# Weights of a two-layer mixer in half tiles: three half places for raw weights, five for low halves, and a low half made from the high half

## The chip, the cores and the metric

The kernel runs on one core of a Trainium2 chip. The metric is the device time of one execution in microseconds. Five engines work side by side and wait for each other by semaphores: TensorE (PE, with its weight loads as PEld), VectorE (DVE), ScalarE (ACT), GpSimd (POOL) and SyncE (SP). Besides them, DMA engines move data between memory and the core; the DMAs of this kernel are issued from the queues of SP and POOL.

## The reference, cut to what matters

Two layers, each of three sublayers with a residual: a gated feed-forward (FFN), a mixing sublayer (Mix), a second FFN. Sequence 512, width 1024, FFN width 2816, all in float32.

```python
for l in range(DEPTH):
    h = swiglu_ffn(rmsnorm(x, ffn1_pre_g[l]), ffn1_w_gu[l], ffn1_w_down[l])
    x = x + 0.5 * rmsnorm(h, ffn1_post_g[l])
    h = mixing_sublayer(rmsnorm(x, mix_pre_g[l]), w_in[l], ...)
    x = x + rmsnorm(h, mix_post_g[l])
    h = swiglu_ffn(rmsnorm(x, ffn2_pre_g[l]), ffn2_w_gu[l], ffn2_w_down[l])
    x = x + 0.5 * rmsnorm(h, ffn2_post_g[l])

def mixing_sublayer(h, ...):
    z = h @ w_in
    uv, pz, qz, kz, vz, qi, ki, wi, cz, gz = jnp.split(z, ...)
    branches = (gmlp_mixer(uv, ...), pool_mixer(pz, ...),
                sparse_attention(qz, kz, vz, qi, ki, wi, rel_bias), conv_mixer(cz, ...))
    gates = jax.nn.sigmoid(gz.reshape(B, S, N_BRANCH, D_MODEL))
    y = sum over n of gates[:, :, n] * (branches[n] @ w_branch[n])
    return y @ w_out

def conv_mixer(ab, dw, db, ln_g, ln_b):      # 31 taps, causal, one filter for each of 256 channels
    a, gt = jnp.split(ab, 2, axis=-1)
    h = a * jax.nn.sigmoid(gt)
    h = lax.conv_general_dilated(h, dw[:, None, :], padding=[(CONV_K - 1, 0)], ...) + db
    return jax.nn.silu(layernorm(h, ln_g, ln_b))
```

## The kernel before

**Products in three parts.** TensorE multiplies in a reduced float32 format. So each operand is split into a high half, the value rounded to that format, and a low half, what is left; a product is wH·xH + wL·xH + wH·xL. The activations lie with features on 128 partitions and the 512 positions along the free axis: eight tiles xH and eight xL. A weight is a tile of 128x1024, eight 128x128 blocks; with it goes one `gemm` (L263) of 24 matmuls of 512 columns, in the order of `mm3s` (L241): for the first seven blocks wH·xH and wL·xH by turns, then wH·xL, then the last block. Thus the first matmul with the low half is the second of the gemm. All of them are recorded with line L253, whatever the stage; the matmuls of the first four weights of a sublayer, its head, have L287.

**Weights.** Each of some 400 weights comes in through `weights()` (L180). SP issues the load of the raw tile (L184) into one of two places of the pool "raw", each 128x1024; ACT copies it to the high half wH (L197). For the low half wL there are three ways:

- in the FFNs, and for the first two gemms behind the head (`ahead_weight`) and the last four of Mix, VectorE subtracts: wL = raw − wH (L202);
- with `far=True`, ACT copies the raw tile with a scale of −1 into wL (L199), which rounds it to the negated high half, and a DMA from POOL's queue adds the weight from memory onto it (L200), which leaves the low half. The tile of the low half is complete when this adding DMA lands. So are made: the weights of Mix behind the head (`col`, L629: positions, gates), the branch weights `w_branch`, the first half of `w_out`, and weights 1 to 3 of a head that follows a sublayer boundary;
- with `ring=True`, the first weight of such a head: two tiles of 128x512 each for high and low half out of the pool "h"; POOL subtracts (L191).

wH has four places of 128x1024 and wL four. A place is free again when the last matmul that reads it has ended.

**Gates.** In `gates` (L749) the four branches follow each other in the order 1, 0, 3, 2. For each of eight output tiles one gate weight (24 matmuls) and two blocks of a branch weight (6 matmuls) go through TensorE; one branch weight serves four output tiles, and so holds its places for four rounds. VectorE normalises the gate's result (L756), ACT makes a tanh of it (L757), VectorE multiplies with the branch's result (L766) and POOL or VectorE adds (L768).

**Beside it.** The attention (scores, top-k on VectorE in L934 and L935, softmax on ACT in L953 to L959, L984), the convolution (31 operations a channel tile on VectorE, L865) and the other branches are generators; `pump` runs a piece of them at each gemm. `conv` works on the tile "cv" of 512 + 30 columns, whose first 30 POOL sets to zero (L699). At a sublayer boundary VectorE makes statistics (L300 to L322) for a matmul (L330) that all of the next scaling waits for.

**What sets the order.** The Python code records instructions in the order of a plan; a list scheduler then sets the order of each engine's queue by its own estimates, keeping data and buffer dependencies. In stretches marked `pinned` the weights keep program order (`pin`, L205). An engine works off its queue strictly in order.

Of the kernel before, what the change touches and what calls it, by code (L numbers as in the profile page):

```python
# [11 lines left out]
F32 = mybir.dt.float32  # L12
F32R = mybir.dt.float32r
I32 = mybir.dt.int32
AF = mybir.ActivationFunctionType
ALU = mybir.AluOpType
AX = mybir.AxisListType

P = 128
N = 512  # L20
# [29 lines left out]
class Builder:  # L50
# [65 lines left out]
    def late_consts(self):  # L116
# [13 lines left out]
        oh = self.t([P, 1024], F32, "raw", 2)  # L130
# [8 lines left out]
    def late_consts2(self):  # L139
        nc, sb, dr = self.nc, self.sb, self.a["rlin"]  # L140
        rev = self.t([P, 4, 256], F32, "raw", 2)
        nc.sync.dma_start(rev, bass.AP(tensor=dr.tensor, offset=dr.offset, ap=[[1, P], [384, 4], [1, 256]]))
        anti = self.tmp(w=P)
        nc.gpsimd.memset(anti, 0.0)
        nc.gpsimd.affine_select(out=anti, in_=anti, pattern=[[1, P]], compare_op=ALU.not_equal, fill=1.0,
                                base=-(P - 1), channel_multiplier=1)
        self.tb = sb.tile([P, 4, 256], F32, name="tb")
        for j in range(2):
            pj = self.pt("st")
            nc.tensor.matmul(pj, anti, rev[:, 2 * j:2 * j + 2, :], start=True, stop=True)  # L150
            nc.scalar.activation(self.tb[:, 2 * j:2 * j + 2, :], pj, AF.Copy)
# [27 lines left out]

    def weights(self, src, n, ring=False, raw=None, far=False):  # L180

        nc = self.nc
        raw = raw or self.t([P, 1024], F32, "raw", 2)
        nc.sync.dma_start(raw[:, :n], src)  # L184
        if ring:
            hs, ls = [], []
            for i in range(2):
                h, lo = self.ring(), self.ring()
                r = raw[:, i * N:(i + 1) * N]
                nc.scalar.activation(h, r, AF.Copy)  # L190
                nc.gpsimd.tensor_tensor(lo, r, h.bitcast(F32), op=ALU.subtract)  # L191
                hs.append(h)
                ls.append(lo)
            return hs, ls
        h = self.t([P, 1024], F32R, "wH", 4)
        lo = self.t([P, 1024], F32R, "wL", 4)
        self.pin(nc.scalar.activation(h[:, :n], raw[:, :n], AF.Copy))  # L197
        if far:
            self.pin(nc.scalar.activation(lo[:, :n], raw[:, :n], AF.Copy, scale=-1.0))  # L199
            nc.gpsimd.dma_start(lo[:, :n], src, accum_op=ALU.add)  # L200
            return h, lo
        self.pin(nc.vector.tensor_tensor(lo[:, :n], raw[:, :n], h.bitcast(F32)[:, :n], op=ALU.subtract))  # L202
        return h, lo
# [362 lines left out]
class Mix:  # L566
# [33 lines left out]
    def params(self):  # L600
        b, nc, l, a = self.b, self.b.nc, self.l, self.b.a

        raw = b.t([P, 1024], F32, "raw", 2)
# [16 lines left out]
        raw = b.t([P, 1024], F32, "raw", 2)  # L620
# [30 lines left out]
    def rest(self):  # L651
# [42 lines left out]
        for j in range(2):  # L694
            zg = self.norm(T_CZ + 2 + j)
            nc.scalar.activation(zg, zg, AF.Tanh, scale=0.5)
            za = self.norm(T_CZ + j, scale=0.5)
            hp = b.t([P, N + CONV_K - 1], F32, "cv", 2)
            nc.gpsimd.memset(hp[:, 0:CONV_K - 1], 0.0)  # L699
            nc.vector.scalar_tensor_tensor(hp[:, CONV_K - 1:], zg, 1.0, za, op0=ALU.add, op1=ALU.mult)  # L700
            self.hpad.append(hp)
# [152 lines left out]
    def conv(self):  # L854
# [3 lines left out]
        for j in range(2):  # L858
# [3 lines left out]
            nc.vector.tensor_scalar(a, hp[:, 0:N], dw(0), b.v(l, V_CB + j), op0=ALU.mult, op1=ALU.add)  # L862
            yield 450
            for t in range(1, CONV_K):
                nc.vector.scalar_tensor_tensor(a, hp[:, t:t + N], dw(t), a, op0=ALU.mult, op1=ALU.add)  # L865
                if t % 2 == 0:
                    yield 1360
# [200 lines left out]
```

## Time and profile before

| | us |
|---|---|
| median of 3 runs (2332.76 to 2336.97) | 2333.0 |
| the profiled execution, its own time | 2332.65 |
| its span, first to last instruction | 2330.9 |
| PE busy | 2283.6 |
| DVE busy | 1193.7 |
| ACT busy | 927.4 |
| POOL busy | 276.6 |

The first layer takes roughly 0 to 380 us (FFN1), 380 to 790 (Mix) and 790 to 1165 (FFN2), the second 1165 to 1545, 1545 to 1950 and 1950 to 2331. The busy time of an engine is a sum over its instructions; the queries by stage and by wait tell where TensorE stands still and for whom. "x <- y" in a wait means that x stood until y had ended. A DMA's row shows its issue; when it lands is given apart.

### The profile page before, as it was taken

Reading aid. Unit: us, or ns where it says so; the run is one execution under the profiler, and the core shown is the slowest. Engines: PE = TensorE matmul, PEld = TensorE weight load, DVE = VectorE, ACT = ScalarE, POOL = GpSimd, SP = SyncE. Lnnn points to the kernel's source line nnn. Section 1 sums busy time; section 2 is a strip of 40 time slices with the busy share of each in tenths; the row PEclk is TensorE's granted clock in tenths of the full one; section 3 lists DMA queues with packets and bytes.
Section 4 is the critical chain, followed back from the end, with each engine's and each line's share of the span. In section 5 each row is a group of like instructions: output and inputs, shape, how many; then the busy total and the mean of one; then the engine's idle time right before and its main releaser. Section 6 shows DMA issues by size and latency. Waiting matters only on the chain.

```text
span 2330.9 us, 28353 instructions
## 1 busy us (share of the span) xinstructions
PE 2283.6 (98%) x11158; PEld 1909.0 (82%) x11158; DVE 1193.7 (51%) x2144; ACT 927.4 (40%) x1390; POOL 276.6 (12%) x326
## 2 busy tenths in 40 slices
PE   8999999999999999999999999999999999999997
PEld 7888889777888988888888888887778889888886
DVE  5333346799433552433573334468984336423345
ACT  5232224564554532222343222355545545322221
POOL 0000003311331200000110000032123312000001
PEclk9999999999999999999999999999999999999999
DMA  5333333867778433233333323347687773323322
GB/s 170 100 99 92 108 92 90 188 145 168 178 166 182 115 100 98 92 99 97 99 105 93 111 91 100 91 114 167 145 181 174 173 169 100 104 95 95 99 91 68
DMA packets 82557, 282.27 MB, mean 121 GB/s; under 512 B 9428, under 2 KB 13176, under 8 KB 82424
## 3 DMA queue, kind: packets, MB, share of 16 engines
q1 hardware_dynamic: 64136, 213.87, 28.5%
q0 software_dynamic: 18288, 66.59, 16.7%
q8 instruction: 87, 1.43, 0.2%
q14 instruction: 46, 0.38, 0.1%
HBM read 278.32 MB, written 2.10 MB: 120 GB/s over the span
## 4 chain that ended last, share of the span: by engine, by line
PE 85%; DVE 9%; ACT 2%; issue 2%; DMA 1%; POOL 0%; SPq 0%; POOLq 0%; DVEq 0%; ACTq 0%
PE mm L253 49%; PE at L253 31%; DVE ca L865 3%; PE mm L287 2%; PE at L287 1%; DMA wL<-in_w_in_dram 1%; DVE sc L935 1%; DVE t L402 1%; DVE m L934 1%; PE st L330 1%; PE st L314 1%; DVE x L405 1%; DVE xL L416 1%; ACT wH L197 0%; DVE t L646 0%
## 5 line engine op out<-in xcount | busy, mean ns | idle before, releaser
L197 ACT ACTIVATE wH<-raw 128x1024 fp32r<-128x1024 f32 (+1 forms) x394 | 407.4, 1037 | 836.8 <-issue 581.7
L253 PE MATMUL mm<-xH,wL 128*128 128x512 f32 x1344 | 525.9, 392 | 6.5 <-DMA wL<-in_w_in_dram 6.5
L253 PE MATMUL mm<-xH,wH 128*128 128x512 f32 x1344 | 530.5, 396 | 1.6 <-DVE t L756 1.3
L202 DVE TENSOR_TENSOR wL<-raw,wH 128x1024 fp32r<-128x1024 f32 (+1 forms) x272 | 324.3, 1194 | 255.9 <-ACT wH L197 255.7
L253 PE MATMUL mm<-h,wH 128*128 128x512 f32 (+1 forms) x1496 | 409.2, 354 | 0.3 <-DVE t L756 0.3
L253 PE MATMUL mm<-xL,wH 128*128 128x512 f32 x1344 | 359.0, 389 | 0.0
L253 PEld LDWEIGHTS mm<-xH,wL 128*128 128x128 f32 x1344 | 253.4, 189 | 61.7 <-DMA wL<-in_w_in_dram 9.4
L253 PEld LDWEIGHTS mm<-xH,wH 128*128 128x128 f32 x1344 | 253.3, 188 | 58.5 <-issue 4.2
L253 PEld LDWEIGHTS mm<-h,wH 128*128 128x128 f32 x1496 | 263.8, 188 | 41.8 <-DVE t L756 0.5
L253 PEld LDWEIGHTS mm<-xL,wH 128*128 128x128 f32 x1344 | 252.5, 188 | 52.6
L253 PE MATMUL at<-xH,wH 128*128 128x512 f32 x704 | 277.1, 395 | 7.3 <-ACT xH L223 6.7
L253 PE MATMUL at<-xH,wL 128*128 128x512 f32 x704 | 274.0, 391 | 0.0
L253 PE MATMUL mm<-h,wL 128*128 128x512 f32 (+1 forms) x748 | 252.4, 352 | 0.0
L253 PE MATMUL at<-h,wH 128*128 128x512 f32 (+1 forms) x776 | 219.6, 366 | 0.0
L199 ACT ACTIVATE wL<-raw 128x1024 fp32r<-128x1024 f32 x122 | 128.6, 1054 | 176.9 <-PE mm L253 144.9
L253 PE MATMUL at<-xL,wH 128*128 128x512 f32 x704 | 187.8, 389 | 0.0
L253 PEld LDWEIGHTS at<-xH,wH 128*128 128x128 f32 x704 | 132.9, 189 | 37.6 <-ACT xH L223 7.0
L253 PEld LDWEIGHTS at<-h,wH 128*128 128x128 f32 x776 | 140.4, 188 | 24.6
L253 PEld LDWEIGHTS mm<-h,wL 128*128 128x128 f32 x748 | 140.4, 188 | 20.3
L253 PEld LDWEIGHTS at<-xH,wL 128*128 128x128 f32 x704 | 132.7, 188 | 29.3 <-issue 1.4
L253 PEld LDWEIGHTS at<-xL,wH 128*128 128x128 f32 x704 | 132.2, 188 | 27.5
L253 PE MATMUL at<-h,wL 128*128 128x512 f32 (+1 forms) x388 | 136.5, 366 | 0.0
(212 smaller groups left out, 2300.8 us busy)
## 6 DMA issues: line engine op xcount, KB each, us to landing
raw<-in_ffn_w_gu_dram SPq DMA_DIRECT2D x173, 512.0 KB, 3.5
raw<-in_w_in_dram SPq DMA_DIRECT2D x98, 512.0 KB, 6.4
wL<-in_w_in_dram POOLq DMA_DIRECT2D x94, 512.0 KB, 7.1
raw<-in_ffn_w_down_dram SPq DMA_DIRECT2D x64, 448.0 KB, 3.3
raw<-in_ffn_w_down_dram SPq DMA_DIRECT2D x32, 512.0 KB, 3.5
raw<-in_w_branch_dram SPq DMA_DIRECT2D x16, 512.0 KB, 5.1
wL<-in_w_branch_dram POOLq DMA_DIRECT2D x16, 512.0 KB, 7.0
raw<-in_w_out_dram SPq DMA_DIRECT2D x16, 512.0 KB, 6.5
```

Source lines behind the costliest of these rows:

```text
L197: self.pin(nc.scalar.activation(h[:, :n], raw[:, :n], AF.Copy))
L199: self.pin(nc.scalar.activation(lo[:, :n], raw[:, :n], AF.Copy, scale=-1.0))
L202: self.pin(nc.vector.tensor_tensor(lo[:, :n], raw[:, :n], h.bitcast(F32)[:, :n], op=ALU.subtract))
L253: self.nc.tensor.matmul(out, w[a], m[b], start=(first and i == 0), stop=(last and i == 3 * n - 1))
L287: self.nc.tensor.matmul(out, w[a], m[b], start=(count[j] == 1), stop=(count[j] == 3 * KD))
L314: self.nc.tensor.matmul(ps[:, c - c0:c - c0 + 1], s[:, c * P:(c + 1) * P], self.ones[:, 0:1], start=(i == 0), stop=(i == len(tiles) - 1))
L330: self.nc.tensor.matmul(ps[:, s], self.ones, dg[:, s], start=True, stop=True)
L402: nc.vector.scalar_tensor_tensor(u[:, c], s.o[k][:, c], self.v(s.post[0], s.post[1] + k), pb[:, c], op0=ALU.mult, op1=ALU.mult)
L405: e.tensor_tensor(self.xt[k][:, c], self.xt[k][:, c], u[:, c], op=ALU.add)
L416: nc.vector.scalar_tensor_tensor(self.xl[k][:, c], self.xt[k][:, c], g, self.xh[k].bitcast(F32)[:, c], op0=ALU.mult, op1=ALU.subtract)
L865: nc.vector.scalar_tensor_tensor(a, hp[:, t:t + N], dw(t), a, op0=ALU.mult, op1=ALU.add)
L934: nc.vector.max(m8, sc[:, :W])
```

## The change

Raw weights land in half tiles: the pool "raw" has three places of 128x512 in place of two of 128x1024. A weight is then two loads, two copies to wH and, where VectorE subtracts, two subtractions. With `far`, one negation of the whole tile reads wH, no longer the raw tile, so that it comes behind both copies; the adding DMA is unchanged. The ring's low halves are made likewise by ACT and adding DMAs. wL has five places, wH still four. The convolution's tile has no padding and no memset; a tap s works on 512 − s columns. The bias constants (`late_consts2`) land in two half tiles.

```diff
+    def raw(self):
+        return self.t([P, N], F32, "raw", 3)
+
     def weights(self, src, n, ring=False, raw=None, far=False):
 
         nc = self.nc
-        raw = raw or self.t([P, 1024], F32, "raw", 2)
-        nc.sync.dma_start(raw[:, :n], src)
+        cs = [slice(c, min(c + N, n)) for c in range(0, n, N)]
         if ring:
-            hs, ls = [], []
-            for i in range(2):
-                h, lo = self.ring(), self.ring()
-                r = raw[:, i * N:(i + 1) * N]
-                nc.scalar.activation(h, r, AF.Copy)
-                nc.gpsimd.tensor_tensor(lo, r, h.bitcast(F32), op=ALU.subtract)
-                hs.append(h)
-                ls.append(lo)
+            hs, ls = [self.ring() for _ in cs], [self.ring() for _ in cs]
+        else:
+            h = self.t([P, 1024], F32R, "wH", 4)
+            lo = self.t([P, 1024], F32R, "wL", 5)
+            hs, ls = [h[:, c] for c in cs], [lo[:, c] for c in cs]
+        if raw is not None:
+            nc.sync.dma_start(raw[:, :n], src)
+        for c, hc, lc in zip(cs, hs, ls):
+            r = raw[:, c] if raw is not None else self.raw()[:, :c.stop - c.start]
+            if raw is None:
+                nc.sync.dma_start(r, src[:, c])
+            self.pin(nc.scalar.activation(hc, r, AF.Copy))
+            if ring or far:
+                continue
+            self.pin(nc.vector.tensor_tensor(lc, r, hc.bitcast(F32), op=ALU.subtract))
+        if ring:
+            for c, hc, lc in zip(cs, hs, ls):
+                nc.scalar.activation(lc, hc.bitcast(F32), AF.Copy, scale=-1.0)
+                nc.gpsimd.dma_start(lc, src[:, c], accum_op=ALU.add)
             return hs, ls
-        h = self.t([P, 1024], F32R, "wH", 4)
-        lo = self.t([P, 1024], F32R, "wL", 4)
-        self.pin(nc.scalar.activation(h[:, :n], raw[:, :n], AF.Copy))
         if far:
-            self.pin(nc.scalar.activation(lo[:, :n], raw[:, :n], AF.Copy, scale=-1.0))
+            self.pin(nc.scalar.activation(lo[:, :n], h.bitcast(F32)[:, :n], AF.Copy, scale=-1.0))
             nc.gpsimd.dma_start(lo[:, :n], src, accum_op=ALU.add)
-            return h, lo
-        self.pin(nc.vector.tensor_tensor(lo[:, :n], raw[:, :n], h.bitcast(F32)[:, :n], op=ALU.subtract))
         return h, lo
...
-            hp = b.t([P, N + CONV_K - 1], F32, "cv", 2)
-            nc.gpsimd.memset(hp[:, 0:CONV_K - 1], 0.0)
-            nc.vector.scalar_tensor_tensor(hp[:, CONV_K - 1:], zg, 1.0, za, op0=ALU.add, op1=ALU.mult)
+            hp = b.t([P, N], F32, "cv", 2)
+            nc.vector.scalar_tensor_tensor(hp, zg, 1.0, za, op0=ALU.add, op1=ALU.mult)
...
-                nc.vector.scalar_tensor_tensor(a, hp[:, t:t + N], dw(t), a, op0=ALU.mult, op1=ALU.add)
+                nc.vector.scalar_tensor_tensor(a[:, s:], hp[:, :N - s], dw(CONV_K - 1 - s), a[:, s:],
+                                               op0=ALU.mult, op1=ALU.add)
```

In the changed kernel the same lines have other numbers: the copy to wH is L202, the negation L212, the adding DMA L213, the subtraction L205, the gate's tanh L767, the softmax L962 to L970, the matmul L264.

ACT's queue in the last branch of the second layer's gates, before. A name's number only tells buffers apart; `wL<-raw` is the negation, `wH<-raw` the copy, `t<-t` of L757 the gate's tanh, `h<-y` the split of a finished output tile.

```order
L223 ACTIVATE h_15087<-y_13428 128x512
L199 ACTIVATE wL_15197<-raw_15194 128x1024
L197 ACTIVATE wH_15196<-raw_15194 128x1024
L757 ACTIVATE t_15123<-t_15123 128x512
L197 ACTIVATE wH_15244<-raw_15242 128x1024
L199 ACTIVATE wL_15245<-raw_15242 128x1024
L223 ACTIVATE h_15135<-y_13523 128x512
L199 ACTIVATE wL_15293<-raw_15290 128x1024
```

The same place of ACT's queue in the changed kernel:

```order
L234 ACTIVATE h_16251<-y_14502 128x512
L202 ACTIVATE wH_16367<-raw_16369 128x512
L202 ACTIVATE wH_16367<-raw_16372 128x512
L767 ACTIVATE t_16290<-t_16290 128x512
L212 ACTIVATE wL_16368<-wH_16367 128x1024
L202 ACTIVATE wH_16418<-raw_16420 128x512
L234 ACTIVATE h_16302<-y_14600 128x512
L202 ACTIVATE wH_16418<-raw_16423 128x512
L212 ACTIVATE wL_16419<-wH_16418 128x1024
```

The negation of a gate's weight has moved from ahead of the copy and the tanh to behind both.

ACT's queue in the second layer's gates of branch 0, beside the convolution, before (L220 splits a result of another branch, L984 one of the attention):

```order
L220 ACTIVATE h_13699<-t_13679 128x512
L199 ACTIVATE wL_13842<-raw_13839 128x1024
L197 ACTIVATE wH_13841<-raw_13839 128x1024
L757 ACTIVATE t_13749<-t_13749 128x512
L199 ACTIVATE wL_13900<-raw_13897 128x1024
```

And in the changed kernel:

```order
L231 ACTIVATE h_14785<-t_14765 128x512
L202 ACTIVATE wH_14934<-raw_14936 128x512
L202 ACTIVATE wH_14934<-raw_14939 128x512
L767 ACTIVATE t_14838<-t_14838 128x512
L212 ACTIVATE wL_14935<-wH_14934 128x1024
```

Here too the tanh, whose input comes from VectorE, now stands ahead of the negation.

POOL's queue in the first layer, where the second convolution tile is made, before:

```order
L200 DMA wL_4133<-in_w_in_dram 128x1024
L200 DMA wL_4202<-in_w_in_dram 128x1024
L699 MEMSET cv_12881 128x30
L200 DMA wL_4268<-in_w_branch_dram 128x1024
L951 TENSOR_TENSOR t_4108<-sc_629_3309,tb 128x256
```

And in the changed kernel:

```order
L213 DMA wL_4467<-in_w_in_dram 128x1024
L213 DMA wL_4539<-in_w_in_dram 128x1024
L213 DMA wL_4608<-in_w_branch_dram 128x1024
L962 TENSOR_TENSOR t_4444<-sc_705_3608,tb 128x256
L962 TENSOR_TENSOR t_4455<-sc_705_3608,tb 128x256
```

The memset between the adding DMAs is gone; their order is the same.

## Rows read from the trace of the kernel before

**Rows 1.** The page: busy time by engine, and the chain that ended last.

```profile
PE 2283.6 (98%) x11158; PEld 1909.0 (82%) x11158; DVE 1193.7 (51%) x2144; ACT 927.4 (40%) x1390; POOL 276.6 (12%) x326
...
PE 85%; DVE 9%; ACT 2%; issue 2%; DMA 1%; POOL 0%; SPq 0%; POOLq 0%; DVEq 0%; ACTq 0%
```

**Rows 2.** Windows: stretch, its length, busy PE, PEld, DVE, ACT, POOL, clock, DMA.

```profile
16.00:440.00 424.00, 421.44 (x2040) 351.20 (x2039) 195.12 (x308) 148.35 (x216) 24.33 (x30) 1.00 0.37 108
440.00:960.00 520.00, 510.36 (x2490) 424.44 (x2489) 298.79 (x604) 249.29 (x386) 100.59 (x115) 0.99 0.59 143
```

**Rows 3.** Waits of TensorE, whole span: total us, times, longest us.

```profile
PE st L330 <- DVE t L322: 10.5, 6, 2.4
...
PE mm L253 <- DMA wL<-in_w_in_dram: 6.5, 5, 3.8
...
PE at L969 <- ACT t L959: 1.7, 1, 1.7
PE mm L253 <- DVE t L756: 1.7, 2, 1.3
```

**Rows 4.** Timeline of PE: start, duration, operation, in the last gates of layer 2.

```profile
1880.42 0.47 PE L253 MATMUL mm<-xH,wL 128*128 128x512 f32 x1
```

**Rows 5.** Timeline of ACT there; in brackets the idle time ahead and its end.

```profile
1871.89 1.06 ACT L199 ACTIVATE wL<-raw 128x1024 fp32r<-128x1024 f32 x1 [2.24 <-PE mm L253]
1872.86 1.04 ACT L197 ACTIVATE wH<-raw 128x1024 fp32r<-128x1024 f32 x1
1873.80 0.61 ACT L757 ACTIVATE t<-t 128x512 f32<-128x512 f32 x1
1874.32 1.04 ACT L197 ACTIVATE wH<-raw 128x1024 fp32r<-128x1024 f32 x1
```

**Rows 6.** Timeline of POOL at two adding DMAs of layer 2's gates.

```profile
1834.37 0.88 POOL L200 DMA_DIRECT2D wL<-in_w_in_dram  x1 [3.35 <-ACT wL L199]
...
1873.24 0.86 POOL L200 DMA_DIRECT2D wL<-in_w_in_dram  x1 [6.04 <-PE mm L253]
```

**Rows 7.** DMA issues, us to landing: the one at 1834.37, the one at 1873.24.

```profile
wL<-in_w_in_dram POOLq DMA_DIRECT2D x1, 512.0 KB, 5.4
...
wL<-in_w_in_dram POOLq DMA_DIRECT2D x1, 512.0 KB, 7.1
```

**Rows 8.** Groups by form, ACT and DVE: count, busy us, mean ns, idle before.

```profile
L197 ACT ACTIVATE wH<-raw 128x1024 fp32r<-128x1024 f32 x330 | 346.3, 1053 | 597.9 <-issue 392.8 <-PE mm L253 60.6 <-DMA raw<-in_ffn_w_gu_dram 52.2
...
L202 DVE TENSOR_TENSOR wL<-raw,wH 128x1024 fp32r<-128x1024 f32 x208 | 254.4, 1225 | 234.9 <-ACT wH L197 234.8
L221 DVE TENSOR_TENSOR h<-t,h 128x512 fp32r<-128x512 f32 x106 | 73.1, 690 | 2.8 <-ACT h L220 2.3
```

**Rows 9.** The page's DMA issues: count, KB each, median us to landing.

```profile
raw<-in_ffn_w_gu_dram SPq DMA_DIRECT2D x173, 512.0 KB, 3.5
...
wL<-in_w_in_dram POOLq DMA_DIRECT2D x94, 512.0 KB, 7.1
```

**Rows 10.** Timeline of SP's queue beside the two adding DMAs of rows 6.

```profile
1836.36 0.33 SPq L184 DMA_DIRECT2D raw<-in_w_in_dram  x1
...
1873.92 0.33 SPq L184 DMA_DIRECT2D raw<-in_w_in_dram  x1
```

**Rows 11.** Timeline of ACT in the second layer's gates beside the convolution.

```profile
1675.78 1.04 ACT L199 ACTIVATE wL<-raw 128x1024 fp32r<-128x1024 f32 x1
...
1680.61 0.63 ACT L757 ACTIVATE t<-t 128x512 f32<-128x512 f32 x1 [2.83 <-DVE t L756]
...
1712.15 1.04 ACT L199 ACTIVATE wL<-raw 128x1024 fp32r<-128x1024 f32 x1
...
1715.72 0.63 ACT L757 ACTIVATE t<-t 128x512 f32<-128x512 f32 x1 [1.58 <-DVE t L756]
```

**Rows 12.** Timeline of POOL in the first layer's convolution.

```profile
513.57 0.13 POOL L699 MEMSET cv<- 128x30 f32 x1 [6.50 <-DVE ca L865]
514.07 0.84 POOL L200 DMA_DIRECT2D wL<-in_w_branch_dram  x1 [0.37 <-issue]
```

More of the change, by code (lines that the diff above doesn't have):

```diff
@@ L129, in late_consts @@
         nc.sync.dma_start(self.rb31, bass.AP(tensor=rbh.tensor, offset=rbh.offset + 31 * 4, ap=[[0, P], [1, 4]]))
-        oh = self.t([P, 1024], F32, "raw", 2)
+        oh = self.raw()
         nc.sync.dma_start(oh[:BUCKETS, :384], a["onehot"])
@@ L140, in late_consts2 @@
         nc, sb, dr = self.nc, self.sb, self.a["rlin"]
-        rev = self.t([P, 4, 256], F32, "raw", 2)
-        nc.sync.dma_start(rev, bass.AP(tensor=dr.tensor, offset=dr.offset, ap=[[1, P], [384, 4], [1, 256]]))
+        rev = [self.raw() for _ in range(2)]
+        for j, r in enumerate(rev):
+            nc.sync.dma_start(r.rearrange("p (h k) -> p h k", h=2),
+                              bass.AP(tensor=dr.tensor, offset=dr.offset + 2 * j * 384,
+                                      ap=[[1, P], [384, 2], [1, 256]]))
         anti = self.tmp(w=P)
@@ L149, in late_consts2 @@
             pj = self.pt("st")
-            nc.tensor.matmul(pj, anti, rev[:, 2 * j:2 * j + 2, :], start=True, stop=True)
+            nc.tensor.matmul(pj, anti, rev[j], start=True, stop=True)
             nc.scalar.activation(self.tb[:, 2 * j:2 * j + 2, :], pj, AF.Copy)
@@ L601, in params @@
         b, nc, l, a = self.b, self.b.nc, self.l, self.b.a
-        raw = b.t([P, 1024], F32, "raw", 2)
+        raw = b.raw()
         nc.sync.dma_start(raw[:, :512], a["gm_ws"][l])
@@ L618, in params @@
         nc.sync.dma_start(self.vg, bass.AP(tensor=g.tensor, offset=g.offset + l * C, ap=[[0, P], [1, C]]))
-        raw = b.t([P, 1024], F32, "raw", 2)
+        raw = b.raw()
         nc.sync.dma_start(raw[:, :256], a["pool_w"][l])
@@ L861, in conv @@
             dw = lambda t: b.v(l, V_DW + t * 2 + j)
-            nc.vector.tensor_scalar(a, hp[:, 0:N], dw(0), b.v(l, V_CB + j), op0=ALU.mult, op1=ALU.add)
+            nc.vector.tensor_scalar(a, hp, dw(CONV_K - 1), b.v(l, V_CB + j), op0=ALU.mult, op1=ALU.add)
             yield 450
-            for t in range(1, CONV_K):
-                nc.vector.scalar_tensor_tensor(a, hp[:, t:t + N], dw(t), a, op0=ALU.mult, op1=ALU.add)
-                if t % 2 == 0:
+            for s in range(1, CONV_K):
+                nc.vector.scalar_tensor_tensor(a[:, s:], hp[:, :N - s], dw(CONV_K - 1 - s), a[:, s:],
+                                               op0=ALU.mult, op1=ALU.add)
+                if s % 2 == 0:
                     yield 1360
```

## The prediction

> **What bounds the kernel now.** I read the page first: TensorE is busy 2283.6 of 2330.9 us, and the chain of work that ended last is 85% TensorE, 9% VectorE and 1% DMA [rows 1]. So only what lies under 47 us of TensorE idle time can be won. The windows by stage come next: in 16 to 440 us, nearly all feed-forward work, TensorE idles 2.6 us in 424; in 440 to 960, which holds the Mix stage, 9.6 in 520 [rows 2]. TensorE's own waits say what it lacks [rows 3]: 10.5 us for the statistics at the boundaries (VectorE, L322), 6.5 us in five waits for the DMA that completes a low half (wL), 1.7 us each for a softmax operation (L959) and the first VectorE operation of a gate (L756). None of these names the subtraction L202. So the feed-forward weights are early, and the change can act only through the low halves that are made by ACT and a DMA: those of Mix.
>
> There the reader must see one weight's road, for example that of the matmul at 1880.42 [rows 4]. ACT negates the raw weight at 1871.89, after a wait that a matmul ended, the last to read the place's former weight; the high half follows at 1872.86 and the gate's tanh at 1873.80 [rows 5]. GpSimd issues the adding DMA at 1873.24 [rows 6] and it lands 7.1 us later [rows 7], at 1880.34, 0.1 us before the matmul of the low half. Laid out this way for all 107 weights of the two Mix stages, 19 have under 1.8 us to spare. These are what the change is about.
>
> **The change part by part.** *Half tiles.* A 128x1024 copy on ACT takes 1053 ns [rows 8], but ACT starts an instruction before the one ahead has ended: 1874.32 − 1873.80 = 0.52 us after a 512-wide one, 1872.86 − 1871.89 = 0.97 after a 1024-wide one [rows 5], so two halves cost 1.04, +0.07. On VectorE a subtraction takes 1225 ns, one of half the width 690 [rows 8]: 2×690 − 1225 = +155 ns for 272 weights, some 40 us of a VectorE that idles half of the span. Feed-forward weights land after 3.5 us [rows 9] and none is waited for; cover is there, price 0. Were it gone, 0.155 + 0.07 us on 272 weights would be 61 us; [rows 2, 3] speak against it.
>
> *The negation waits for the high half.* Before, it stood ahead of the high half and started when the low half's place came free. The place of a high half comes free one matmul (0.23 us) later, and both halves of the copy, and in most gates the tanh, now stand ahead of the negation in ACT's order: 0.23 + 2×0.52 + 0.52 = 1.8 us later. The fifth place does not help: the negation reads the high half, of which there are still four places, and branch and gate weights free both halves at the same matmul. So the fifth place costs and gives 0, unless a weight's high half is waiting already.
>
> *A shorter adding DMA.* The raw tile is now free after the copies, not after the negation, so SP issues the next half loads sooner: the first half is free some 0.6 us after its copy starts, and the adding DMA is issued 2×0.52 + 0.52 + 1.06 + 0.29 = 2.9 us after that start, so the loads go out about 2.3 and 1.8 us ahead of it instead of beside or behind it. Behind the DMA of 1873.24 a raw load was issued at 1873.92, and the DMA took 7.1 us [rows 6, 7, 10]; at 1834.37 the next raw load came only at 1836.36, and it took 5.4 [rows 6, 7, 10]. So an adding DMA that has the engines to itself saves up to 1.7 us. With the loads 2 us ahead, most of their 3.5 us [rows 9] has passed: I take 1.2 of the 1.7, bounds 0 and 1.7.
>
> The Trainium skill, "DMA: Bandwidth & Descriptors", section "Issuing engines are not separate DMA queues", says that transfers started by different engines run on the same DMA engines and interleave, whichever began them. The two adding DMAs agree with it, 7.1 against 5.4 us [rows 7]; by that rule alone the same bytes must still move, and the saving would be near 0, which is the first rival below.
>
> *Sum over the gates.* A weight with no time to spare moves 1.8 − 1.2 = 0.6 us. With its own 0.1 us to spare taken off, 0.5 is left at 721.6 and at 1880.4; at 531.9 the tanh waits for VectorE besides, 0.7. Where no tanh stands between (574.2) it is 0, and the others have more to spare than 0.6. Together **+1.7**.
>
> *Gates beside the convolution.* While VectorE is late (convolution and top-k), the tanh waits for it, and the negation now behind it. At 1675.78 the negation stood ahead of a tanh that started at 1680.61; it will start at 1681.1, 5.3 later, 4.1 with the shorter DMA. For the one negated at 1712.15 the tanh came at 1715.72, so the negation 4.1 later, its landing 2.9 [rows 11]. The first has 0.1 us to spare, but TensorE waits for VectorE and the softmax at 1692.7 (1.7), 1695.8 (about 1) and 1706.2 (1.3) anyway [rows 3], waits whose ends VectorE and ACT set; the 4.1 shrinks to about 0.5. The second meets no such wait before 1740: +2.9. Together **+3.4**, bounds 0 (if VectorE reaches these gates some 4 us earlier) and 7 (if the first is not taken up).
>
> *Convolution without padding.* The memset on GpSimd waited 6.50 us for the convolution's tile and held the adding DMA behind it until 514.07 [rows 12]. That weight is used 26 us later; the weight of the wait at 531.9 was negated at 523.6, behind the softmax. Worth 0, upper bound 3.8, that wait, the longest of its kind [rows 3]. Narrower taps (mean 496.5 of 512) save 16 ns each on VectorE, 2 us in 120, off the path.
>
> *Boundaries and start.* The GpSimd subtractions of a head's first weight become two negations on ACT and two DMAs; its low half comes late in that head. The boundary wait is VectorE's statistics, the same operations in the same order: 0. At the start, loads limit TensorE whatever their width; finer halves could move the first matmul 0.7 us either way. Together 0 ± 1.
>
> Sum: 1.7 + 3.4 = +5.1 on the profiled 2332.65 us (span 2330.9 and 1.75 around it; the median of the runs is 2333.0): **2338.0 us**.
>
> **The rivals.** *No saving in the DMA.* The 1.8 us stay whole. Weight by weight, shortfalls are 1.7 (504.1), 1.5 (531.9), 1.0 (574.2), 1.7 (721.6), 0.8 (749.6), 1.4 (1684.0), 1.4 (1720.3), 1.1 (1873.5), 0.5 (1880.4), 1.0 (1901.6) and five of 0.1 to 0.3: 13.0, so 2346. For it: most of the adding DMAs in the trace have a load beside them and a median of 7.1 [rows 9]. Against it: the 5.4 above.
>
> *Nothing reaches the path.* The shorter DMA saves the whole 1.7, and the convolution's gates are taken up by the waits behind them: 2333 to 2335. For it: just 0.1 us lies between 1.8 and 1.7.
>
> *Faster: low halves stop being last.* The price is the waits that go: 6.5 us for wL [rows 3], so 2326. It decides where the raw halves land earlier and the place is free already: if a weight's high half does not wait for its place, then the negation follows directly and the DMA, shorter by 1.7, lands early. It needs more than 1.8 us gained per weight. Against it: the negation waited for the matmul that freed the place [rows 5], and the order puts the high half and the tanh ahead of it.
>
> **How the numbers follow.** Of this kernel a measurement tells 0.2%, 4.7 us, from no change: faster is under 2328.3, slower over 2337.7. The forecast, 5.1 with a reach of 3 to 9, has 0.42, of which 0.27 lie above the line; the whole 1.8 has 0.18, all slower; nothing on the path 0.25, of which 0.03 reach below the line; low halves no longer last 0.15, of which 0.12 are faster. So slower 0.45, same 0.40, faster 0.15. The range leaves out a tenth at each end: from 2328 (most of the faster case is outside) to 2347 (the first rival's 13 and the start's 1).
>
> **What would show it.** Right: the negation starts about 1.8 us after the wait for the place ends, with the tanh ahead; adding DMAs have a median near 6 us; TensorE's waits for wL grow from 6.5 to some 8 to 12 us; the wait for wL at 1720 is near 3 us. Wrong if the DMAs stay at 7.1 (first rival), if ACT's high halves wait for a raw half in Mix (the half loads are then last, which I price at 0), if feed-forward stages wait for L205, or if TensorE's wait for wL falls to about 0 (the last rival).

## The result

The changed kernel takes 2357.06 us (median of 4 runs, 2354.09 to 2358.89) against 2332.88 for the kernel before (2331.46 to 2336.97): a ratio of 1.0095, 95% interval 1.0075 to 1.0115. It is 24 us slower. The forecast was 2338.0 with a range of 2328 to 2347; the direction was the one held likeliest, the size was not in the range.

The profiled execution took 2354.09 us, the shortest of the four; its span is 2352.3, 21.4 us over the span before, so that its trace holds 21 of the 24 us. The page after, engines and chain, beside [rows 1]:

```profile
PE 2290.8 (97%) x11158; PEld 1913.6 (81%) x11158; DVE 1211.7 (52%) x2416; ACT 979.2 (42%) x1799; POOL 267.6 (11%) x322
...
PE 78%; issue 7%; DVE 5%; DMA 5%; ACT 2%; POOL 1%; POOLq 0%; SPq 0%; DVEq 0%; ACTq 0%
```

TensorE runs the same 11158 matmuls. It idles 2352.3 − 2290.8 = 61.5 us where it idled 47.3, and is busy 7.2 us longer with the same work. DMA has gone from 1% of the chain to 5%. The waits of TensorE, to be held against [rows 3]:

```profile
PE mm L264 <- DMA wL<-in_w_in_dram: 17.9, 11, 5.2
...
PE at L298 <- ACT xH L421: 6.6, 4, 2.6
...
PE mm L264 <- DVE t L766: 2.2, 3, 1.9
```

The waits for adding DMAs nearly tripled, 6.5 us to 17.9. A wait that the prediction priced at nothing has grown: heads of sublayers wait 6.6 us for the high half of the activations. Before, it was 1.6:

```profile
PE at L287 <- ACT xH L410: 1.6, 5, 0.4
```

Since both kernels run the same matmuls in nearly the same order, the clearest view is a ledger worked out from the two traces: the start of the k-th matmul after, minus its start before. Where this offset steps, time was lost.

| place (us in the trace before) | offset after the place | step |
|---|---|---|
| start, up to 100 | +0.9 | +0.9 |
| FFN1, 100 to 378 | +0.95 | 0 |
| head of Mix, 378 to 392 (up to +4.0, then back) | +1.1 | +0.1 |
| behind the head, 418 to 423 | +2.85 | +1.8 |
| Mix of layer 1, 423 to 760 | +8.1 | +5.2 |
| boundary at 797 | +8.5 | +0.5 |
| boundary at 1165 | +11.0 | +2.4 |
| boundary at 1535 | +12.4 | +1.4 |
| behind the head, 1574 to 1580 | +14.15 | +1.7 |
| Mix of layer 2, 1580 to 1912 | +21.8 | +7.7 |
| boundary at 1948, end | +21.3 | −0.5 |

In sum 12.9 in the two Mix stages behind the heads, 7.9 at the heads and right behind them, 0.9 at the start and −0.5 at the end. The 0.9 of the start tells little: there the traces of the thirteen experiments lie 0.1 to 2.5 us behind the kernel before. In the feed-forward stages the offset stands still.

**A gate in the changed kernel.** ACT's timeline at the gate that answers to [rows 5] (start, duration, operation, and in brackets the idle time ahead), and POOL's adding DMA of that weight, beside [rows 6]:

```profile
1892.58 1.15 ACT L202 ACTIVATE wH<-raw 128x512 fp32r<-128x512 f32 x2 [3.10 <-PE mm L264]
1893.64 0.61 ACT L767 ACTIVATE t<-t 128x512 f32<-128x512 f32 x1
1894.16 1.04 ACT L212 ACTIVATE wL<-wH 128x1024 fp32r<-128x1024 f32 x1
```

```profile
1895.49 0.86 POOL L213 DMA_DIRECT2D wL<-in_w_in_dram  x1 [6.03 <-ACT wL L212]
```

and TensorE's wait that it ends:

```profile
1902.19 0.50 PE L264 MATMUL mm<-xH,wL 128*128 128x512 f32 x1 [0.99 <-DMA wL<-in_w_in_dram]
```

The copy waits 3.10 us for the matmul that frees the high half's place, and the negation follows 1.58 us after the copy began: 0.23 + 1.58 = 1.8, as reckoned. The DMA is issued at 1895.49 and lands 6.7 us later; TensorE, which has waited 0.99 us for it, goes on at 1902.19.

**Behind a wait.** The windows of the changed kernel about the wait of 1736.4 (stretch, length, busy PE, PEld, DVE, ACT, POOL, granted clock, DMA share, GB/s):

```profile
1729.00:1734.00 5.00, 5.00 (x23) 4.11 (x22) 5.00 (x14) 2.73 (x4) 0.86 (x1) 1.00 0.30 52
1734.00:1736.40 2.40, 0.42 (x3) 0.02 (x1) 2.40 (x7) 0.28 (x1) 0.00 (x0) 1.00 0.99 244
1736.40:1739.80 3.40, 3.40 (x9) 2.63 (x10) 3.40 (x11) 3.37 (x5) 0.85 (x1) 0.54 0.39 114
```

TensorE idled about 2 of 2.4 us, and in the 3.4 us behind that the granted clock is 0.54, close to the lower of the two levels (1.2 of 2.4 GHz). Matmuls start 0.43 us apart there instead of 0.23. Adding up the excess of all such runs of four matmuls or more gives about 6 us in the kernel before and about 12 in the changed one (an estimate from the starts of the matmuls; a us or two hang on the pace that one calls slow): some 6 us of the 21.3, and most of the longer busy time.

**At a boundary.** ACT's timeline of the changed kernel at the boundary of 1165:

```profile
1172.10 0.61 ACT L202 ACTIVATE wH<-raw 128x512 fp32r<-128x512 f32 x1
1174.54 0.63 ACT L202 ACTIVATE wH<-raw 128x512 fp32r<-128x512 f32 x1 [1.83 <-DMA raw<-in_ffn_w_gu_dram]
1175.20 1.06 ACT L212 ACTIVATE wL<-wH 128x1024 fp32r<-128x1024 f32 x1
1176.17 1.69 ACT L421 ACTIVATE xH<-x,vec 128x256 fp32r<-128x256 f32 x4
```

and the same place before, where the whole tile had landed:

```profile
1163.46 1.05 ACT L197 ACTIVATE wH<-raw 128x1024 fp32r<-128x1024 f32 x1
1164.41 1.05 ACT L199 ACTIVATE wL<-raw 128x1024 fp32r<-128x1024 f32 x1
1165.36 1.78 ACT L410 ACTIVATE xH<-x,vec 128x256 fp32r<-128x256 f32 x4
```

With three half places one and a half weights can be under way instead of two. The second half of the head's last weight is loaded late, its copy waits 1.83 us at the head of ACT's queue, and the last four splits of the activations, which TensorE waits for, stand behind it. Over the whole span ACT's copies waited for loads of w_in 25.5 us in 18 places:

```profile
ACT wH L202 <- DMA raw<-in_w_in_dram: 25.5, 18, 2.7
```

Before, the copies waited 6.0 us in 2 places, but the negations, which then stood ahead of the copies, 31.0 in 11:

```profile
ACT wL L199 <- DMA raw<-in_w_in_dram: 31.0, 11, 5.4
...
ACT wH L197 <- DMA raw<-in_w_in_dram: 6.0, 2, 3.0
```

So ACT did not wait longer for these loads than before. But the low halves of those eleven negations still landed 4.4 to 9.6 us ahead of their use; now such a wait can stand ahead of something that TensorE needs at once, as here. What the half places cost is told by the runs below and not by these sums.

### The profile page after: what moved, and what is told of

It reads as the page before. It is cut to its first block, busy times and chain, and to the rows that moved or that the text cites. A ratio compares the mean times of both kernels' runs of the same rounds, so it can differ in the third digit from the quotient of the medians.

```text
span 2352.3 us, 30204 instructions
## 1 busy us (share of the span) xinstructions
PE 2290.8 (97%) x11158; PEld 1913.6 (81%) x11158; DVE 1211.7 (52%) x2416; ACT 979.2 (42%) x1799; POOL 267.6 (11%) x322
## 4 chain that ended last, share of the span: by engine, by line
PE 78%; issue 7%; DVE 5%; DMA 5%; ACT 2%; POOL 1%; POOLq 0%; SPq 0%; DVEq 0%; ACTq 0%
PE mm L264 44%; PE at L264 30%; DMA wL<-in_w_in_dram 3%; PE at L298 2%; PE mm L298 2%; DMA raw<-in_w_in_dram 1%; POOL wL L213 1%; ACT wH L202 1%; DVE ca L875 1%; DMA raw<-in_ffn_w_gu_dram 1%; DVE sc L946 1%; DVE m L945 1%; ACT wL L212 1%; PE st L341 0%; PE st L325 0%
## 5 line engine op out<-in xcount | busy, mean ns | idle before, releaser
L202 ACT ACTIVATE wH<-raw 128x512 fp32r<-128x512 f32 (+1 forms) x788 | 453.5, 615 | 1023.3 <-issue 602.6
L264 PE MATMUL mm<-xH,wL 128*128 128x512 f32 x1344 | 529.9, 395 | 18.1 <-DMA wL<-in_w_in_dram 17.9
L264 PE MATMUL mm<-xH,wH 128*128 128x512 f32 x1344 | 533.0, 398 | 0.3 <-DVE t L766 0.3
L205 DVE TENSOR_TENSOR wL<-raw,wH 128x512 fp32r<-128x512 f32 (+1 forms) x544 | 345.5, 673 | 181.8 <-ACT wH L202 179.3
L264 PE MATMUL mm<-h,wH 128*128 128x512 f32 (+1 forms) x1496 | 408.8, 353 | 1.9 <-DVE t L766 1.9
L264 PE MATMUL mm<-xL,wH 128*128 128x512 f32 x1344 | 359.3, 389 | 0.0
L264 PEld LDWEIGHTS mm<-xH,wL 128*128 128x128 f32 x1344 | 255.3, 190 | 77.0 <-DMA wL<-in_w_in_dram 23.8
L264 PEld LDWEIGHTS mm<-xH,wH 128*128 128x128 f32 x1344 | 255.2, 190 | 57.8 <-issue 4.0
L264 PEld LDWEIGHTS mm<-h,wH 128*128 128x128 f32 x1496 | 263.7, 188 | 43.2 <-DVE t L766 2.1
L264 PEld LDWEIGHTS mm<-xL,wH 128*128 128x128 f32 x1344 | 252.1, 188 | 52.3
L264 PE MATMUL at<-xH,wH 128*128 128x512 f32 x704 | 276.6, 395 | 9.0 <-ACT xH L234 9.0
L264 PE MATMUL at<-xH,wL 128*128 128x512 f32 x704 | 273.7, 391 | 0.0
L264 PE MATMUL mm<-h,wL 128*128 128x512 f32 (+1 forms) x748 | 252.3, 352 | 0.0
L264 PE MATMUL at<-h,wH 128*128 128x512 f32 (+1 forms) x776 | 219.5, 366 | 0.0
L264 PE MATMUL at<-xL,wH 128*128 128x512 f32 x704 | 187.8, 389 | 0.0
L264 PEld LDWEIGHTS at<-xH,wH 128*128 128x128 f32 x704 | 132.8, 189 | 38.7 <-ACT xH L234 9.0
L264 PEld LDWEIGHTS at<-h,wH 128*128 128x128 f32 x776 | 140.4, 188 | 24.6
L264 PEld LDWEIGHTS mm<-h,wL 128*128 128x128 f32 x748 | 140.4, 188 | 20.5 <-DMA wL<-in_w_out_dram 0.2
L264 PEld LDWEIGHTS at<-xH,wL 128*128 128x128 f32 x704 | 132.7, 188 | 29.1 <-issue 1.4
L264 PEld LDWEIGHTS at<-xL,wH 128*128 128x128 f32 x704 | 132.1, 188 | 27.5
L264 PE MATMUL at<-h,wL 128*128 128x512 f32 (+1 forms) x388 | 136.4, 366 | 0.0
L487 DVE TENSOR_TENSOR t<-at,t 128x512 f32<-128x512 f32 x60 | 41.5, 692 | 182.5 <-PE at L264 178.6
```

The lines of the kernel that those rows point to most:

```text
L202: self.pin(nc.scalar.activation(hc, r, AF.Copy))
L205: self.pin(nc.vector.tensor_tensor(lc, r, hc.bitcast(F32), op=ALU.subtract))
L264: self.nc.tensor.matmul(out, w[a], m[b], start=(first and i == 0), stop=(last and i == 3 * n - 1))
L487: nc.vector.tensor_tensor(hp, pb, a1, op=ALU.mult)
```

## Experiments

Theory A: the loss of Mix comes from the negation that waits for the high half, because a high half has four places; each new wait then costs some lower clock besides. Theory B: the three half places for raw weights are behind nearly all of it. Theory C: half-wide operations cost by themselves. All runs were compared with the kernel before on the same chip; its medians lay between 2333.2 and 2335.2 us.

### The late negation alone, and the places of raw weights

The first run is the kernel before with one line changed:

```diff
-            self.pin(nc.scalar.activation(lo[:, :n], raw[:, :n], AF.Copy, scale=-1.0))
+            self.pin(nc.scalar.activation(lo[:, :n], h.bitcast(F32)[:, :n], AF.Copy, scale=-1.0))
```

> The kernel before with one line changed: the negation reads the high half instead of the raw tile; raw tiles stay two of 128x1024, low halves four places. Theory A (the late negation costs the gates, and lower clock follows each new wait): the negation starts 0.23 + 0.95 + 0.52 = 1.7 us later in gates, as in the changed kernel, so Mix loses what it lost there, 13 us in the ledger of TensorE starts (5 in the first layer, 8 in the second), and the boundaries lose nothing: about 2344 us, between 2340 and 2348. Theory B (three half places for raw weights cost nearly everything, in Mix too, because loads come late): within 2 us of the kernel before, 2333. Theory C (the half-width operations themselves): 2333 too.

Measured 2349.0 us, ratio 1.0059 (1.0041 to 1.0077). ACT's timeline at the gate of [rows 5], then TensorE's wait for adding DMAs:

```profile
1893.34 1.06 ACT L197 ACTIVATE wH<-raw 128x1024 fp32r<-128x1024 f32 x1 [2.26 <-PE mm L253]
1894.31 0.62 ACT L757 ACTIVATE t<-t 128x512 f32<-128x512 f32 x1
1894.83 1.04 ACT L199 ACTIVATE wL<-wH 128x1024 fp32r<-128x1024 f32 x1
```

```profile
PE mm L253 <- DMA wL<-in_w_in_dram: 20.6, 12, 5.6
```

With whole tiles and nothing else changed, the negation is as late, and the waits for adding DMAs rise to 20.6 us. The ledger of this run has +6.9 in the first Mix, +7.2 in the second, +0.5 from 760 to 1580 (and +1.5 at the start). So theory A holds for Mix, and B and C, which expected 2333, do not hold as the chief cause. The loss was 1 us over the range that theory A gave.

Next, the changed kernel with four half places for raw weights, and its bytes from the low halves, and, since the fifth low place is in that comparison too, the changed kernel with four low places alone:

```diff
-        return self.t([P, N], F32, "raw", 3)
+        return self.t([P, N], F32, "raw", 4)
...
-            lo = self.t([P, 1024], F32R, "wL", 5)
+            lo = self.t([P, 1024], F32R, "wL", 4)
```

> The changed kernel with four half places for raw weights (the same bytes as before) and four places for low halves. Theory A: the waits of the boundaries for ACT's xH (6.6 us in 4) go, and with them some lower clock, 4 to 6 us; the gates stay as slow as in the changed kernel: 2350 to 2353 us. Theory B: nearly the whole loss goes, 2333 to 2340. If the fifth place for low halves had been worth something, the gates would get slower than in the changed kernel.

> The changed kernel with four places for low halves instead of five. If the fifth place is worth nothing, since the high half binds: as the changed kernel, 2354 to 2359 us. If the fifth place held down the loss: 2360 or more. Together with the run with four half places for raw weights and four for low halves (2351.8) it gives the price of the third-against-fourth raw place alone.

Measured 2351.8 us with four raw places (ratio 1.0069), 2360.6 with three (1.0109, 1.0094 to 1.0124). The fourth half place is worth 8.8 us with four low places. And the fifth low place, which the prediction had at 0, comes to 2360.6 − 2357.1 = 3.5 us while there are three half places, 2 of them in the ledger right behind the first head; but the intervals of the two ratios (1.0094 to 1.0124, 1.0075 to 1.0115) overlap, so it may be less.

To have the raw place alone, the bytes were taken elsewhere: once from the pool "h" (19 of 20 places), once from "t" (11 of 12), with five low places as in the change.

> The changed kernel with four half places for raw weights and five for low halves still, 19 for h. Three against four half places cost 8.8 us with four low places (2360.6 against 2351.8). If that holds with five low places: 2346 to 2350 us, the rest over the kernel before being the late negation, as in the run with that alone (2349.0). If the fifth low place and the fourth raw place cover the same waits: 2351 to 2355.

> The changed kernel with the fourth half place for raw and nothing else but 11 places of t for its bytes (five low, four high). In the run with 19 places of h it gave 2354.8, with the same wait for the ring's DMAs (5.0 us). Without that wait: 2347 to 2351, which would be the late negation alone (2349.0) and would make the third-against-fourth raw place 6 to 10 us. If 2353 to 2356, the raw places are worth at most 4 us here and the rest of the loss has another cause.

With 19 places of h: 2354.8 us, ratio 1.0085 (1.0070 to 1.0101); with 11 of t: 2349.6, ratio 1.0068 (1.0050 to 1.0086). TensorE's waits, first with h cut, then with t cut, and ACT's wait for loads of w_in with t cut:

```profile
PE at L298 <- DMA h<-in_ffn_w_gu_dram: 5.0, 2, 2.5
...
PE at L298 <- ACT xH L421: 3.0, 5, 0.7
```

```profile
PE mm L264 <- DMA wL<-in_w_in_dram: 20.1, 14, 5.2
...
PE at L298 <- ACT xH L421: 2.0, 3, 0.7
```

```profile
ACT wH L202 <- DMA raw<-in_w_in_dram: 2.5, 4, 0.9
```

The first of the two was a poor experiment: the missing place of h made the ring's new adding DMAs late, a wait of 5.0 us that stands in neither kernel. Without it the fourth half place gives back 2357.1 − 2349.6 = 7.4 us (6 by the ratios, whose intervals overlap a little; with four low places they do not, and the 8.8 are clear of the noise). The heads' waits fall from 6.6 to 2.0 us, the copies' waits for loads of w_in from 25.5 to 2.5, and what is left is what the late negation costs alone (2349.0). The change is thus two losses: some 15 us by the negation, some 7 by the raw places.

### The place that binds

If four high places make the late negation dear, a fifth must cure it. The changed kernel with the fifth place moved from low to high halves:

```diff
-            h = self.t([P, 1024], F32R, "wH", 4)
-            lo = self.t([P, 1024], F32R, "wL", 5)
+            h = self.t([P, 1024], F32R, "wH", 5)
+            lo = self.t([P, 1024], F32R, "wL", 4)
```

> The changed kernel with the fifth place given to the high halves instead of the low halves (same bytes). Theory A: the copies no longer wait for the high half's place, the negation can start when the low half's place comes free, so the loss of the gates goes in large part (8 to 12 of 13 us); boundaries stay: 2343 to 2350 us. Theory B and C: as the changed kernel, 2354 to 2359.

Measured 2363.5 us (1.0119, 1.0098 to 1.0140): slower, where 2343 to 2350 was expected. The ledger of its profiled execution (2367.8, the longest of the four) shows both: between 500 and 800 its offset falls from +17.7 to +15.1, and from 1740 to the end it stays at +35, so there the gates lose nothing any more. But right behind the heads it steps by 9 us (418) and 8 (1574), and from 1590 to 1740 it still rises by 7, mostly in waits for VectorE. ACT's and VectorE's timeline there:

```profile
419.96 0.63 ACT L202 ACTIVATE wH<-raw 128x512 fp32r<-128x512 f32 x1 [3.17 <-DMA raw<-in_w_in_dram]
422.98 0.63 ACT L202 ACTIVATE wH<-raw 128x512 fp32r<-128x512 f32 x1 [2.39 <-DMA raw<-in_w_in_dram]
423.52 0.58 ACT L374 ACTIVATE rb__641_3342<-st 128x512 f32<-128x512 f32 x1
```

```profile
424.13 1.29 DVE L657 TENSOR_TENSOR t<-at,rb__641_3342 128x512 f32<-128x512 f32 x2 [11.17 <-ACT rb__641_3342 L374]
```

Since a high place is free, the scheduler puts copies earlier, ahead of the copy of the row scales (L374) that every later operation of Mix needs; and the copies wait for half loads that three places let out one after the other. VectorE stands 11.17 us, where it stood 4.7 in the kernel before. That is the raw places' cost again, in a worse spot. With whole tiles it should not be there: the kernel with the late negation alone, five high places, and 19 places of h.

> The kernel before with the negation from the high half (as in the run that gave 2349) and five places for high halves; the pool h gives up one of its 20 places for the bytes. If four high places are what makes the late negation cost the gates, that loss goes: Mix at most 3 us over the kernel before, so 2331 to 2337 us, unless the missing place of h costs by itself. If something else in the late negation costs, such as ACT's order, it stays near 2349.

Measured 2334.7 us, ratio 1.0002 (0.9992 to 1.0011), and no step behind the heads in the ledger. TensorE's waits, then ACT's timeline at the gate of [rows 5]:

```profile
PE mm L287 <- ACT wH L197: 3.5, 2, 2.0
PE mm L253 <- DMA wL<-in_w_in_dram: 3.0, 4, 1.2
```

```profile
1869.96 1.06 ACT L199 ACTIVATE wL<-wH 128x1024 fp32r<-128x1024 f32 x1 [2.24 <-PE mm L253]
1870.92 1.05 ACT L197 ACTIVATE wH<-raw 128x1024 fp32r<-128x1024 f32 x1
1871.87 0.61 ACT L757 ACTIVATE t<-t 128x512 f32<-128x512 f32 x1
```

One more high place takes the late negation from 2349.0 to 2334.7, and the waits for adding DMAs from 20.6 us to 3.0, half of what the kernel before has. This is the sharpest of the runs. The negation still reads the high half, but a free high place lets the copy go a round earlier, and the negation heads the queue again: it waits 2.24 us for a matmul that frees its place, with the copy and the tanh behind it, just as in [rows 5]. So reading the high half costs nothing by itself; what costs is the negation standing behind a copy that has no place yet. The 3.5 us of the heads came from h; with t cut instead:

> As the run that gave 2334.7 (negation from the high half, five high places, whole raw tiles), but the bytes come from the pool t (11 places of 12) and h keeps 20. The waits of a head for its first high half (3.5 us in two) should go, if they came from h: 2329 to 2333 us. If t binds: 2340 or more.

Measured 2330.8 us (12 runs) against 2335.2, ratio 0.9982 (0.9971 to 0.9992): a version faster than both kernels, by a little.

### Both causes out

The changed kernel with four half places, five high and four low, the bytes first from h, then from t:

> The changed kernel with four half places for raw weights, five places for high and four for low halves, 19 for h. If the late negation behind four high places and the three half places are the two causes, both are gone: Mix's gates as in the kernel before or faster, boundaries as in the kernel before, and Mix's start without the waits for half loads that stood ahead of the statistics' copy on ACT in the run with three half places: 2332 to 2340 us. If half tiles cost by themselves (more loads and copies), 2345 or more.

> As the run that gave 2342.4 (four half places for raw, five high, four low), but the bytes come from t (11 places) and h keeps 20. In that run a head waited 4.4 us for the ring's new adding DMAs, which stood behind the missing place of h. If that is all that was left: 2334 to 2339 us, and half tiles cost by themselves no more than that over the whole-tile kernel with the same places (2330.8). If half tiles cost more, 2341 to 2345.

With h cut 2342.4 us (1.0034, 1.0021 to 1.0047), again with a wait for the ring's DMAs, 4.4 us in two; with t cut 2337.5 (1.0010, 0.9996 to 1.0023), not told from the kernel before. Its waits:

```profile
PE mm L264 <- DMA wL<-in_w_in_dram: 1.9, 2, 1.0
```

Half tiles, the new ring and the other convolution together are thus not free here: 2337.5 against 2330.8 for the whole-tile kernel with the same places, and the intervals of the two ratios do not meet. Between the two traces the starts of the matmuls step by 4.1 us right behind the first head and by 4.0 behind the second, 6.9 in all (of profiled executions that took 2341.5 and 2334.5). There a copy waits for a half load ahead of L374 once more:

```profile
416.95 0.63 ACT L202 ACTIVATE wH<-raw 128x512 fp32r<-128x512 f32 x1 [1.65 <-DMA raw<-in_w_in_dram]
417.49 0.58 ACT L374 ACTIVATE rb__641_3342<-st 128x512 f32<-128x512 f32 x1
```

With four high places the rest is 3 us at most: 2349.6 and 2351.8 with half tiles (four raw places, five and four low), 2349.0 with whole ones. Half-wide operations and the ring were not run by themselves, so what share of the 6.7 us is theirs stays open.

### The other ways to a low half, and the convolution

Would the negation from the raw tile have been better in the changed kernel? Each half is negated from its raw half:

```diff
+            if far:
+                self.pin(nc.scalar.activation(lc, r, AF.Copy, scale=-1.0))
             if ring or far:
                 continue
...
-            self.pin(nc.scalar.activation(lo[:, :n], h.bitcast(F32)[:, :n], AF.Copy, scale=-1.0))
```

> The changed kernel, but each half of a far weight is negated from its raw half tile, so that the negation need not follow the copy. Theory A: in the gates the negation is early again and the loss of Mix (13 us) mostly goes, the boundaries stay slow: 2342 to 2348 us. Theory B: no gain, since raw places are now held until the negation too: 2355 to 2362. Theory C: slightly slower than the changed kernel, since a negation is two operations now (122 times 0.07 us on ACT).

Measured 2405.7 us (1.0302): theory A's 2342 to 2348 was far off. ACT's waits between 440 and 790:

```profile
ACT wL L204 <- DMA raw<-in_w_in_dram: 76.4, 33, 5.0
```

The low place is free early, so a negation is taken early, but its raw half then stays taken until the copy, which waits for a high place; the next half load comes late, and the next negation waits for it at the head of ACT's queue, ahead of tanh and softmax. That is read off more easily in the kernel before, with nothing but a fifth low place (and 19 places of h):

```diff
-        lo = self.t([P, 1024], F32R, "wL", 4)
+        lo = self.t([P, 1024], F32R, "wL", 5)
```

> The kernel before, negation from the raw tile, with five places for low halves and 19 for h. The negation waits for nothing but its own place, so a fifth place lets it start one gemm sooner, unless the raw tile is then held too long by the copy behind it. By that, the five waits for adding DMAs (6.5 us) go: 2326 to 2330 us. If the raw tile or the high half's place binds: 2333, and if the raw tile is held longer and the next load is late: 2336 and more.

Measured 2452.0 us (1.0501, 1.0485 to 1.0517), 119 us slower. ACT's wait for raw loads, and its timeline at 619:

```profile
ACT wL L199 <- DMA raw<-in_w_in_dram: 289.4, 72, 7.6
```

```profile
619.46 1.06 ACT L199 ACTIVATE wL<-raw 128x1024 fp32r<-128x1024 f32 x1 [6.31 <-DMA raw<-in_w_in_dram]
620.42 1.04 ACT L197 ACTIVATE wH<-raw 128x1024 fp32r<-128x1024 f32 x1
621.37 0.61 ACT L757 ACTIVATE t<-t 128x512 f32<-128x512 f32 x1
628.01 1.06 ACT L199 ACTIVATE wL<-raw 128x1024 fp32r<-128x1024 f32 x1 [6.02 <-DMA raw<-in_w_in_dram]
```

In these rounds ACT stands some 6 us in front of a load that could not start sooner (the one that ends the wait ahead of 628.01 is issued at 621.49, as the copy of 620.42 ends and frees its place), and the gate's tanh waits behind it. The missing place of h is not the cause: the run of 2334.7 us had 19 places too. What the expectation lacked is a price: it named the late load and put "2336 and more" to it, with no bound. One more place of one kind is not worth a little or nothing; it can move the wait to an engine's queue.

The convolution of the change alone, in the kernel before:

> The kernel before with the convolution of the changed one alone: no padding, no memset, narrower taps. Prediction's own term: 0, so 2333 (2331 to 2335). If the memset carried the wait at 531.9: 2329.

Measured 2335.7 us (2331.96 to 2341.73), ratio 1.0007 (0.9996 to 1.0018): no difference that can be told.

## Why the prediction was wrong

**Where the change acts.** That "the change can act only through the low halves" of Mix was the first step to fail; it put the raw half places at 0. The rows showed what TensorE waited for before; they do not show the waits one engine further back. ACT waited for loads of w_in, 37.0 us in 13 places, and there was time to spare behind nearly all of them. With three half places there was not: 7.9 us of the ledger lie at heads and right behind them, where "boundaries and start, 0 ± 1" stood, and the fourth half place gives 7.4 us back. The prediction named the sign ("if ACT's high halves wait for a raw half in Mix"), and it came. The row on which the step should have rested is the places themselves: 2 x 1024 columns against 3 x 512.

**The late negation, +5.1.** This term had the right mechanism and a wrong size: it measured 15 us alone (2349.0 against 2333.6), and Mix behind its heads lost 12.9 in the ledger. The four paragraphs that follow say where.

**The negation's delay.** The 1.8 us is what a gate shows that has a tanh and nothing more behind the copy: of the 112 weights with an adding DMA behind the heads of Mix, 36 are negated 1.6 to 2.0 us later, beyond the offset of the ledger. But 25 are later by more than 2.4 us, since other operations of ACT stand between too. The longest wait of all is one of these, at 504.1 in the trace before. ACT's copy and negation of that weight in the changed kernel, and TensorE's wait:

```profile
494.11 1.15 ACT L202 ACTIVATE wH<-raw 128x512 fp32r<-128x512 f32 x2
...
503.94 1.05 ACT L212 ACTIVATE wL<-wH 128x1024 fp32r<-128x1024 f32 x1
```

```profile
511.66 0.79 PE L264 MATMUL mm<-xH,wL 128*128 128x512 f32 x1 [5.20 <-DMA wL<-in_w_in_dram]
```

Softmax operations and their waits for VectorE lie between the two. The negation is 10.8 us later than before, against 4.8 us that this low half had to spare; the first rival's 1.7 us there supposed 0.1. The like happens at 1668.1 (4.6 us to spare, the negation 5.7 us later and its DMA 2.6 longer, a wait of 3.64). Both waits are nearly made up: TensorE had waits soon after them, 3.77 us at 531.9 and 4.0 in three from 1692.7 to 1706.2, that shrank or went.

**The fifth low place, 0.** Right as to what binds (the four high places, by the run with five); with three half places it came to 3.5 us, not clear of the noise.

**The shorter adding DMA.** The median fell from 7.1 us [rows 9] to 6.6 for w_in, and from 7.0 to 5.6 for the branch weights:

```profile
wL<-in_w_in_dram POOLq DMA_DIRECT2D x94, 512.0 KB, 6.6
...
wL<-in_w_branch_dram POOLq DMA_DIRECT2D x16, 512.0 KB, 5.6
```

The 1.2 us was given to all. The 93 DMAs of Mix that had taken 6 us or more became 1.0 us shorter in the mean, and the 19 that had been shorter than that became 0.8 us longer. Two of these had a half load issued within 0.3 us of them now: at 667.6 from 5.2 to 6.9 us, at 1819.8 from 5.6 to 6.9. At these two the negation was later than 1.8 us as well. ACT's timeline of the changed kernel ahead of the first:

```profile
663.03 0.64 ACT L202 ACTIVATE wH<-raw 128x512 fp32r<-128x512 f32 x1 [3.82 <-PE mm L264]
...
665.94 1.04 ACT L212 ACTIVATE wL<-wH 128x1024 fp32r<-128x1024 f32 x1
```

Two operations of the attention and a half of the next weight stand between too: 0.23 + 2.91 = 3.1 us. With 3.4 us to spare, 3.1 + 1.7 are 1.4 too many, and TensorE waited 1.16. At 728.5 and 1880.4 the DMA stayed near 7 (6.8 and 6.7) and nothing came off the 1.8. So "Together +1.7" became some 6 us (2.3 in layer 1 from 574 on, 4.1 in layer 2 from 1727 on): one mean for a saving that went both ways, and one delay for weights behind whose copies more than a tanh stands.

**Gates beside the convolution.** In layer 2 the sum held: +0.5 net from 1660 to 1707 and, at 1720, +2.1 by the wait and +3.7 with the lower clock behind it, for +2.9. The +0.5 is in part luck: TensorE waited at 1668.1, not at 1684.0, where the low half now landed 1.5 us ahead of its use. In layer 1 the same mechanism was seen only at 531.9. From 542 to 574 it cost 3.3 us more: the negation for 542.3 came 8.1 us later, with two splits besides the tanh between it and the copy, and at 557 TensorE waited 1.85 us for VectorE's first operation of a gate (L766), whose waits come to 2.2 us in all with three half places and to 0.2 with four.

**The lower clock.** Every term priced the wait itself. The trace of before had the price of what follows a wait (12 matmuls of 532.5 to 537.2 at half pace, 2.4 us), and it stands in no term; it came to some 6 us.

**Rivals.** "No saving in the DMA" (2346) is the nearest, and still 11 us short, since it knew nothing of the raw places. The "memset" and the convolution were 0 as said, feed-forward stages too. A small slip besides: 2332.65 + 5.1 is 2337.75, and from the median 2338.1; 2338.0 is neither.

## What to carry to other kernels

Count the places of every pool on a weight's road, and ask of an edit which of them binds after it: here the place that was added (low halves) did not, the one that bound (high halves) was not touched, and the one that was cut (raw) began to. An operation that waits at the head of an in-order queue costs whatever stands behind it, so a place more can make a kernel much slower (2333 to 2452 us) if it lets such an operation move forward. An estimate of how late an operation gets must count all that the queue puts ahead of it, weight by weight. Where both kernels run the same matmuls, the ledger of start times finds the places; price a new wait with the slower matmuls behind it.

## What the runs showed of the hardware

A wait of TensorE of 1.98 us was followed by some 3 us at the lower of its two clock levels (granted clock 0.54 in 1736.4 to 1739.8), though it had run at full clock up to the wait and during it; waits of 1.1 us, as that ahead of 736.52, were followed by matmuls 0.23 us apart, at full pace. The length of the wait alone does not decide it: one of 1.85 us ahead of 562.87 in the changed kernel, and one of 2.37 us ahead of 484.65 in the kernel before, were followed by full clock. The window behind the latter:

```profile
484.65:488.00 3.35, 3.35 (x15) 2.79 (x16) 3.35 (x6) 1.22 (x2) 0.85 (x2) 1.00 1.06 219
```

Behind the heads of Mix in the changed kernel, adding DMAs of one size took from 5.1 to 9.5 us. The 21 of up to 5.4 us had no load issued from 1.3 us ahead of them to 1.2 us behind; of the 13 over 7.8 us, twelve had another adding DMA issued within 6 us ahead of them.
